# Cache-key loads tied to the products, a new panel order for the last head of group one, and output product 3 computed for each token group by itself

## The chip, the cores and the metric

The kernel runs on one core of a Trainium2 chip. Five engines work side by side, each with its own in-order instruction queue: TensorE (matrix products into the PSUM banks), VectorE, ScalarE, GpSimd and SyncE. SyncE only issues DMA transfers; ScalarE and GpSimd issue some as well. The metric is the device time of one execution in microseconds (us), as the median of several runs. Before the change it is 2291.69 us (three runs, 2291.46 to 2292.38).

## The reference

One inference step of a one-layer encoder with two kinds of heads. There are 1024 prompt frames of one new stream, and 16 new frames of each of 8 running streams (128 sample rows), with a width of 2048.

1. h = RMSNorm(x), and then one input projection of 2048 to 8 x 1024 columns: query, key, value and gate of eight stick-breaking heads, and query, key, value and gate of eight retention heads, 128 wide each.
2. Stick-breaking attention: z = q.k / sqrt(128); the weight of an earlier key is sigmoid(z) times the product of sigmoid(-z) over all keys that lie between it and the query. The prompt rows attend to earlier prompt rows. Each running stream attends to 1024 cached keys and values and to its own new rows.
3. Retention: rotary query and key, a decay per head, chunks with a carried 128 x 128 state; each running stream reads and updates its own state.
4. Each head's output is normalised, scaled, multiplied by SiLU(gate). Both groups of heads together (2048 wide) go through the output projection w_out (2048 x 2048). Then x + RMSNorm(out).

Everything is in fp32. The new keys, values and states are outputs too.

## The kernel before

**Precision.** A large product is done as three: operands are split into a rounded high part and the rest (`split`, L164: ScalarE makes the high part, L166, VectorE the rest, L167), and high x high, high x low and low x high are added up in PSUM. So each weight block costs a DMA load, one ScalarE and one VectorE instruction, and three matmuls for each tile or piece of tokens.

**Two token groups.** Group one (`gi` 0) holds prompt tiles 0 to 3 and the sample tile, 640 tokens; group two (`gi` 1) holds prompt tiles 4 to 7, 512 tokens. For each group the eight heads are done one after the other. A head has five pieces of projection: `rows` (values and gates of both branches, tokens on the partitions, L443), and four column panels of `project` (L386), each in four chunks of weights: 0 and 1 are query and key of stick-breaking, 4 and 5 those of retention. The list `order` at the end of the head loop says in which order they come: in group one `rows`, `ret_keys` (5), `ret_queries` (4), `attention` (0, then 1). The last head of group one is special: there `attention` calls `project_pair`, which does two panels chunk by chunk, and between the chunks `load_moving` brings in the inputs of group two, because the tiles of group one's inputs come free chunk by chunk when nothing after the pair reads them.

**Jobs and ticks.** Everything that is not a large product is a generator, a `Job`. After each product matmul step the code calls `tick`, which goes on with at most one job that is due; a job's `yield n` asks to be called again n ticks later. The constants `D_...` are such distances, for group one and group two. `drain(job)` runs ticks without products until the job is done. Three jobs go along with the heads: `ret_job` (retention), `sb_job` (stick-breaking of the prompt rows) and `sub` (`decode`, the running streams, only in group one). Each is drained at the place where its successor is made: `ret_job` in `ret_keys`, `sb_job` and `sub` in `attention` once the query panel is there.

**What orders the queues.** The instructions of each engine are ordered at compile time by a planner that takes the earliest instruction of the program whose inputs it reckons ready, so an instruction that depends on nothing can be placed far ahead of where it was written. `pin` and `tied` hold an instruction behind the last product written (`anchor[0]`) in this plan, without any wait on the chip.

**decode (L782).** The running streams' queries meet the cached keys in two sets of four key tiles (`kcT`, 512 KB each, loaded through GpSimd's queue, L794) and, once `rest` has the new key panel, the new keys. After sigmoid, masks, scan and turning the weights, eight tiles of cached values (`vc`, 512 KB each, on SyncE's queue, L834) follow, in two sets (L868). Keys and values share six buffers (`V_BUFS`). `KC_AHEAD` key tiles are loaded ahead, and the loop goes one tile further every `D_ZC` = 23 ticks. The loads of the keys hang on a free buffer only.

**Between the groups.** In the `attention` of group two's first head, `sub` is drained and the pool that holds these buffers is closed; a new pool takes its place for the attention keys of group two.

**retention (L885).** `ret_branch` turns the retention key around and then waits until `rows_in` holds the rotated query. The sample rows' part waits until a set of the decode's scores gives it a place (`with_scores`), at most `N_READ` x 2 ticks.

**Output products.** The output projection is done by a scheme with seven products of half the size (Strassen's): `LEFT[n]` and `RIGHT[n]` name the operands of product n, quarters of the mixed heads (`s_y`), of w_out, or sums of quarters that were made earlier (`s_s`, `s_b`). `left` loads and splits the left operand of a group in eight pieces; `kept(i)` puts the pieces of group one into the first or second quarter of the input tiles that are no longer read. `product(n, nh, groups, sample, ticks)` computes one half of the columns of product n: eight weight blocks, each used for two token tiles of every group named and, with `sample`, for the sample tile (L1182, L1185, L1186). `load_split` is called two blocks ahead in the order that `order_of` lists, and this list has to agree with the order of the calls. `bank` takes a PSUM bank from the rings acc0 and acc1 in turn; the projections use the same two. `collect` then adds the result to output areas. In the first scope, product 5 and one half of product 1 are computed for group one, while the last heads' jobs of group two go on; then the jobs are drained and the pools of the attention are closed. In the second scope come the rest of product 1 for group one, product 1 of group two, 2 for both, 5 for group two, and 3, 6, 7 and 4 for both. Group two's left operand of product 1 hangs on all eight stick-breaking heads, the last of which ends just before. The dictionary `then` says at which product the left operands of a later one begin to load.

Of the kernel before, what the change touches and what calls it, by code (L numbers as in the profile page):

```python
# [21 lines left out]
H = 8  # L22
# [26 lines left out]
D_OUT = 3  # L49
# [8 lines left out]
D_OP = 2  # L58
D_SUM2 = (4, 6, 26)
D_SUM3 = (3, 3, 6)  # L60
MR = 3
AHEAD = 2
HT = KT // 2
# [24 lines left out]
def tile_hybrid_step(  # L88
# [28 lines left out]
    nc = tc.nc  # L117
# [85 lines left out]
    anchor = [None]  # L203

    def tied(ins):

        if phase[0] == 0 and anchor[0] is not None:
            tc.add_manual_dep(
                ins.ins,
                anchor[0].ins.name,  # L210
                mybir.DependencyInfo(mybir.DependencyClass.NoSync, mybir.DependencyReason.SCHED_ONLY),
                reason="tied to the products",
            )

# [242 lines left out]
    with ExitStack() as s1:  # L457
# [324 lines left out]
        def decode(h, qs, rest):  # L782
# [9 lines left out]
            def load_k(m):  # L792
                kc = ip.tile([P, 2, 512], F32, name="kcT", tag="kv", bufs=V_BUFS)
                ready.append((kc, nc.gpsimd.dma_start(kc, cache_k[h, m // 4, m % 4])))  # L794
# [266 lines left out]
        for gi, g in enumerate(GROUPS):  # L1061
# [6 lines left out]
            for h in range(H):  # L1068
# [32 lines left out]
                def attention():  # L1101
                    nonlocal sb_job, sub, ip, loads
                    held = None
                    if (gi, h) == (0, 0):
                        acc = first[2]
                    elif (gi, h) == (0, H - 1):
                        loads = load_moving(after, 0, NB_TOK, from_h)
                        next(loads)
                        acc, held = project_pair(g, mov, (col(0, h), col(1, h)), loads)
                    else:  # L1110
                        acc = project(g, mov, col(0, h))
# [30 lines left out]
                    if gi == 1:  # L1142
                        kp = wp.tile([P, NB_TOK], F32, name="kpast", tag="mr", bufs=MR)
                        nc.sync.dma_start(kp, s_k[h])
                    acc = held or project(g, mov, col(1, h))
# [16 lines left out]
                if (gi, h) == (0, 0):  # L1162
                    order = ret_start, attention
                elif gi == 0 or h < H - 2:
# [25 lines left out]
        ring = [0]  # L1190
# [15 lines left out]
        order_of = iter([(n, nh, k) for n in (5, 1, 1, 2, 5, 3, 6, 7) for nh in range(2) for k in range(HT)] + [(4, 0, k) for k in range(HT)])  # L1206
# [48 lines left out]
        drain(nxt)  # L1255
        Job(collect(1, 0, product(1, 0, (0,), True, D_OUT)), 1)
        drain(ret_job)
# [4 lines left out]
    with ExitStack() as s3:  # L1262
# [78 lines left out]
        def all_of(made):  # L1341
# [5 lines left out]
            (1, 1): ((2, BOTH),), (2, 1): ((5, G1), (3, G0)), (5, 0): ((3, G1),), (3, 0): ((6, BOTH),),  # L1347
# [33 lines left out]
        for n, groups in ((1, G1), (2, BOTH), (5, G1), (3, BOTH), (6, BOTH), (7, BOTH)):  # L1381
# [168 lines left out]
```

## Time and profile before

| | |
|---|---|
| median of 3 runs | 2291.69 us |
| profiled execution | 2289.71 us |
| its span, from the first instruction to the last | 2288.0 us |
| mean granted TensorE clock | 0.991 |
| busy: TensorE, VectorE, ScalarE, GpSimd | 97%, 55%, 40%, 15% |
| DMA, mean over the span | 204 GB/s |

In the profile, PE is TensorE, PEld its weight loads, DVE VectorE, ACT ScalarE, POOL GpSimd, SP SyncE; a q behind a name (SPq) means the queue that issues, not the engine. A row of the order of time reads: start, length, engine, line, operation, out<-in, count, and in brackets the idle time before it with what ended it. A row of waits reads: who waited for whom, us in total, times, longest. Rows of one view that are not neighbours, and rows of different views in one fence, have a line of "..." between them.

### The profile page before, as it was taken

What the parts mean: (1) busy time and instruction counts of PE and PEld (TensorE: products, weight loads), DVE (VectorE), ACT (ScalarE), POOL (GpSimd) and SP (SyncE); (2) the same over time, 40 slices, a digit from 0 to 9 for tenths busy, and PEclk for the clock granted to TensorE, in tenths of its full rate; (3) what the DMA queues carried; (4) which work ended last, traced back from release to release, by engine and by line L of the source; (5) the groups of instructions that cost most, each with busy time, mean ns of one, the idle gap of its engine ahead of it and who ended that gap; (6) DMA issues with size and microseconds to landing.
All of it is one profiled execution on the core that took longest, in us unless ns stands there. A gap on an engine that the chain in (4) does not pass through costs nothing. (4 is left out here: it accounts for less than half of the span.)

```text
span 2288.0 us, 34700 instructions
## 1 busy us (share of the span) xinstructions
PE 2228.4 (97%) x12002; PEld 1889.0 (83%) x12002; DVE 1261.5 (55%) x2708; ACT 920.6 (40%) x1981; POOL 344.2 (15%) x577
## 2 busy tenths in 40 slices
PE   8999899999999999999989999999999999899998
PEld 7888779798888979888768888888888887678886
DVE  5335445354444545356546665756666666546567
ACT  6433233333333333334434343443334445445363
POOL 0021030111202021120202111120302212000020
PEclk9999999999999999999999999999999999999999
DMA  8566557585666658577668778878888767655586
GB/s 283 177 206 178 171 177 210 159 228 169 182 197 175 201 154 236 158 222 221 195 201 228 236 224 244 236 235 227 239 239 238 213 202 203 207 170 183 149 220 174
DMA packets 440048, 467.04 MB, mean 204 GB/s; under 512 B 182592, under 2 KB 298304, under 8 KB 439360
## 3 DMA queue, kind: packets, MB, share of 16 engines
q1 hardware_dynamic: 317632, 304.35, 45.7%
q0 software_dynamic: 28720, 78.41, 12.3%
q10 hardware_dynamic: 93520, 82.07, 11.6%
q8 instruction: 94, 1.54, 0.3%
q14 instruction: 82, 0.67, 0.1%
HBM read 363.77 MB, written 110.36 MB: 207 GB/s over the span
## 5 line engine op out<-in xcount | busy, mean ns | idle before, releaser
L386 PE MATMUL acc<-mh,wh 128*128 128x256 f32 (+2 forms) x1536 | 444.4, 340 | 19.9 <-ACT wh L166 19.8
L443 PE MATMUL accm<-whn,mh 128*128 128x512 f32 x1152 | 452.3, 393 | 0.1
L443 PE MATMUL accm<-wln,mh 128*128 128x512 f32 x1152 | 451.1, 392 | 0.9 <-DVE wln L167 0.9
L443 PE MATMUL accm<-whn,ml 128*128 128x512 f32 x1152 | 451.9, 392 | 0.0
L386 PE MATMUL acc<-ml,wh 128*128 128x256 f32 (+2 forms) x1536 | 447.3, 342 | 0.0
L386 PE MATMUL acc<-mh,wl 128*128 128x256 f32 (+2 forms) x1536 | 446.7, 341 | 0.3 <-DVE wl L167 0.3
L166 ACT ACTIVATE wh<-wr 128x512 fp32r<-128x512 f32 x392 | 246.8, 631 | 494.1 <-PE acc L386 159.0
L167 DVE TENSOR_TENSOR wl<-wr,wh 128x512 fp32r<-128x512 f32 x392 | 268.0, 687 | 307.1 <-ACT wh L166 289.6
L167 DVE TENSOR_TENSOR wln<-wrn,whn 128x512 fp32r<-128x512 f32 x256 | 175.6, 688 | 296.0 <-ACT whn L166 291.7
L166 ACT ACTIVATE whn<-wrn 128x512 fp32r<-128x512 f32 x256 | 160.8, 632 | 410.6 <-PE accm L443 268.9
L386 PEld LDWEIGHTS acc<-mh,wh 128*128 128x128 f32 x1536 | 285.1, 189 | 40.3 <-ACT wh L166 20.8
L386 PEld LDWEIGHTS acc<-mh,wl 128*128 128x128 f32 x1536 | 283.0, 189 | 25.2 <-issue 5.8
L386 PEld LDWEIGHTS acc<-ml,wh 128*128 128x128 f32 x1536 | 281.9, 190 | 19.0 <-DVE ml L172 0.4
L443 PEld LDWEIGHTS accm<-whn,mh 128*128 128x128 f32 x1152 | 216.4, 188 | 45.1 <-DVE kT L462 0.5
L443 PEld LDWEIGHTS accm<-wln,mh 128*128 128x128 f32 x1152 | 216.4, 188 | 44.6 <-DVE wln L167 1.7
L443 PEld LDWEIGHTS accm<-whn,ml 128*128 128x128 f32 x1152 | 216.5, 188 | 43.9 <-issue 0.8
L636 POOL DMA_DIRECT2D be<-s_be x128 | 94.2, 742 | 151.1 <-DMA s_be<-be 128.1
L672 DVE TENSOR_TENSOR_SCAN kp<-kp 128x1152 f32<-128x1152 f32 (+4 forms) x40 | 82.5, 2062 | 48.2 <-POOL kp L667 26.5
L1182 PE MATMUL a<-wh,mh 128*128 128x512 f32 x240 | 95.1, 397 | 6.4 <-ACT wh L166 3.4
L661 POOL TENSOR_SCALAR_AFFINE_SELECT kb<-kb 128x128 f32<-128x128 f32 x64 | 31.0, 498 | 437.4 <-ACT kb L655 436.6
L1186 PE MATMUL a<-wh,ml 128*128 128x512 f32 x240 | 94.9, 395 | 0.0
L1185 PE MATMUL a<-wl,mh 128*128 128x512 f32 x240 | 94.5, 394 | 0.0
(265 smaller groups left out, 2909.0 us busy)
## 6 DMA issues: line engine op xcount, KB each, us to landing
wr<-w_cols SPq DMA_DIRECT2D x256, 256.0 KB, 4.2
wrn<-w_rows SPq DMA_DIRECT2D x256, 256.0 KB, 3.5
kcT<-cache_k POOLq DMA_DIRECT2D x64, 512.0 KB, 7.6
vc<-cache_v SPq DMA_DIRECT2D x64, 512.0 KB, 5.3
wr<-s_b SPq DMA_DIRECT2D x80, 256.0 KB, 3.8
br<-w_out SPq DMA_DIRECT2D x64, 256.0 KB, 4.5
s_b<-br ACTq DMA_DIRECT2D x32, 512.0 KB, 4.7
wr<-w_out SPq DMA_DIRECT2D x64, 256.0 KB, 3.3
```

The source lines that it names most:

```text
L166: nc.scalar.activation(hi, src, AF.Copy),
L167: nc.vector.tensor_tensor(lo, src, hi.bitcast(F32), ALU.subtract),
L386: last = nc.tensor.matmul(a[:, :m], lhs[:, j, :], rhs[w][:, j, o : o + m], start=(w == 0 and j == 0 and n == 0), stop=(w == KT // WQ - 1 a ...
L443: anchor[0] = nc.tensor.matmul(banks[t], lhs[q][:, j, ts], rhs, start=(k == 0 and n == 0), stop=(k == KT - 1 and n == 2),)
L636: q.dma_start(raw[32 * i : 32 * i + 32, :].rearrange("p (k a) -> p k a", a=32), s[:, :, 32 * i : 32 * i + 32].rearrange("k (j b) a -> b (k ...
L661: nc.gpsimd.affine_select(blk, blk, pattern=[[-1, P]], base=0, channel_multiplier=1, compare_op=ALU.is_gt, fill=fill,)
L672: nc.vector.tensor_tensor_scan(rev, rev, rev, 1.0, ALU.mult, ALU.bypass)
L1182: ins = nc.tensor.matmul(a, hi[k][:, ts], wh, start=first, stop=False)
L1185: nc.tensor.matmul(a, hi[k][:, ts], wl, start=False, stop=False)
L1186: anchor[0] = nc.tensor.matmul(a, lo[k][:, ts], wh, start=False, stop=last)
```

## The change

Three parts, and what goes with them:

1. In `decode`, each load of a key tile is made to wait, on the chip, for the product matmul that was the last one written before it (`behind_products`).
2. In the last head of group one, the order is `rows`, `ret_keys`, `attention`. The query panel of stick-breaking is now computed by itself; then `project_pair` does the query of retention (4) together with the key of stick-breaking (1), with group two's inputs loaded meanwhile, and `ret_queries` rotates the former. So `decode` of this head is started ahead of the pair, `sb_job` and `sub` of the head before are drained there, and the rotated query comes after the pair.
3. Output product 3 is computed for group one (without the sample tile) in the first scope, between the first half of product 1 and the second, with its left operand in `kept(0)` in place of the second quarter; group two and the sample tile follow at its old place. Its weight blocks are loaded and split twice, 16 blocks more. The list of weight blocks follows. The ring of PSUM banks starts at 1 instead of 0.

```diff
+    def behind_products(ins):
+        tc.add_manual_dep(
+            ins.ins,
+            anchor[0].ins.name,
+            mybir.DependencyInfo(mybir.DependencyClass.Sync, mybir.DependencyReason.DATA),
+            reason="no sooner than its turn",
+        )
...
-                ready.append((kc, nc.gpsimd.dma_start(kc, cache_k[h, m // 4, m % 4])))
+                ld = nc.gpsimd.dma_start(kc, cache_k[h, m // 4, m % 4])
+                behind_products(ld)
+                ready.append((kc, ld))
...
-                    elif (gi, h) == (0, H - 1):
-                        loads = load_moving(after, 0, NB_TOK, from_h)
-                        next(loads)
-                        acc, held = project_pair(g, mov, (col(0, h), col(1, h)), loads)
...
+                    if (gi, h) == (0, H - 1):
+                        loads = load_moving(after, 0, NB_TOK, from_h)
+                        next(loads)
+                        queries, held = project_pair(g, mov, (col(4, h), col(1, h)), loads)
+                        ret_queries(queries)
                     acc = held or project(g, mov, col(1, h))
...
+                elif (gi, h) == (0, H - 1):
+                    order = rows, ret_keys, attention
...
-        ring = [0]
+        ring = [1]
...
-        order_of = iter([(n, nh, k) for n in (5, 1, 1, 2, 5, 3, 6, 7) for nh in range(2) for k in range(HT)] + [(4, 0, k) for k in range(HT)])
+        FIRST = ((5, 0), (5, 1), (1, 0), (3, 0), (3, 1), (1, 1))
+        LATER = (1, 2, 5, 3, 6, 7)
+        turns = [*FIRST, *((n, nh) for n in LATER for nh in range(2)), (4, 0)]
+        order_of = iter([(n, nh, k) for n, nh in turns for k in range(HT)])
...
+        mine[0, 3] = kept(0)
+        nxt = Job(left(0, 3, *mine[0, 3], wp, "mr", MR), D_OP)
         Job(collect(1, 0, product(1, 0, (0,), True, D_OUT)), 1)
+        drain(nxt)
+        for nh in range(2):
+            Job(collect(3, nh, product(3, nh, (0,), False, D_OUT)), 1)
         drain(ret_job)
...
-            (1, 1): ((2, BOTH),), (2, 1): ((5, G1), (3, G0)), (5, 0): ((3, G1),), (3, 0): ((6, BOTH),),
+            (1, 1): ((2, BOTH),), (2, 1): ((5, G1),), (5, 0): ((3, G1),), (3, 0): ((6, BOTH),),
...
-        for n, groups in ((1, G1), (2, BOTH), (5, G1), (3, BOTH), (6, BOTH), (7, BOTH)):
+        for n, groups in ((1, G1), (2, BOTH), (5, G1), (3, G1), (6, BOTH), (7, BOTH)):
```

## The prediction

> **What bounds the kernel now.** I read the front page first (busy shares, slices, clock), then the table of busy time by stretch at every place where TensorE pauses, then the waits and the order of time around each pause.
>
> ```profile
> span 2288.0 us, 34700 instructions
> PE 2228.4 (97%) x12002; PEld 1889.0 (83%) x12002; DVE 1261.5 (55%) x2708; ACT 920.6 (40%) x1981; POOL 344.2 (15%) x577
> ```
>
> TensorE is busy for 97% of the span. No matmul is added or taken away by the change, so all it can move is idle time and slow clock: 2288.0 - 2228.4 = 59.6 us idle, of which the start and the end are not touched. The stretches (columns: length; busy time and count of each engine; granted clock; DMA share; GB/s):
>
> ```profile
> core 0: us, PE busy (x) PEld busy (x) DVE busy (x) ACT busy (x) POOL busy (x), PEclk, DMA share, GB/s
> 235.00:245.00 10.00, 0.67 (x2) 0.67 (x3) 1.52 (x6) 1.23 (x3) 0.00 (x0) 0.61 0.97 271
> 245.00:255.00 10.00, 10.00 (x62) 10.00 (x62) 5.99 (x13) 2.78 (x7) 0.00 (x0) 0.88 0.46 142
> 1157.80:1170.70 12.90, 5.74 (x70) 2.80 (x69) 4.02 (x16) 4.07 (x9) 0.00 (x0) 0.80 0.77 229
> 1170.70:1178.70 8.00, 8.00 (x25) 6.35 (x26) 4.16 (x7) 2.16 (x5) 0.00 (x0) 0.68 0.71 230
> 1896.90:1900.00 3.10, 0.82 (x3) 0.43 (x3) 1.53 (x3) 2.01 (x5) 2.18 (x4) 0.90 1.10 201
> 1900.00:1903.00 3.00, 3.00 (x11) 2.42 (x10) 1.10 (x3) 0.56 (x2) 0.59 (x2) 0.53 1.05 302
> 1977.80:1984.60 6.80, 0.37 (x3) 0.04 (x1) 3.46 (x10) 2.87 (x8) 0.86 (x2) 0.76 0.94 281
> 1984.60:1988.20 3.60, 3.60 (x9) 2.86 (x10) 2.59 (x8) 1.80 (x6) 0.00 (x0) 0.51 0.66 251
> 2011.40:2015.20 3.80, 0.40 (x3) 0.05 (x1) 1.89 (x6) 3.11 (x7) 0.00 (x0) 1.00 0.86 247
> 2072.00:2092.00 20.00, 20.00 (x90) 16.57 (x89) 15.74 (x29) 16.10 (x38) 0.00 (x0) 1.00 0.71 225
> ```
>
> Five pauses, and behind four of them a stretch at a lower granted clock, which costs (1 - clock) x length. Each part of the change lies next to one or two of them, so I cost it pause by pause.
>
> **Pause one, 235 us: the keys' burst.** Head 0's decode frees the shared cache buffers at its two value products, and the loads of the next head's keys, bound to nothing, go out at once:
>
> ```profile
> 223.72 1.12 POOL L794 DMA_DIRECT2D kcT<-cache_k  x2 [23.58 <-PE pd L868]
> 228.50 2.20 POOL L794 DMA_DIRECT2D kcT<-cache_k  x4 [3.65 <-PE pd L868]
> ...
> 223.49 5.13 SPq L636 DMA_DIRECT2D ro<-s_rk  x4
> 228.72 7.91 SPq L636 DMA_DIRECT2D so<-s_o  x4
> 236.74 0.58 SPq L375 DMA_DIRECT2D wr<-w_cols  x1
> ...
> 1136.09 2.12 SPq L636 DMA_DIRECT2D ro<-s_rk  x4
> 1148.85 1.92 SPq L636 DMA_DIRECT2D so<-s_o  x4
> ```
>
> Six loads of 512 KB in 7 us; in the same time SyncE's queue spends 5.13 + 7.91 = 13.0 us on eight turn-in transfers that take it 2.12 + 1.92 = 4.0 us where no keys are loaded, and the weight block behind them is issued 9.0 us late.
>
> ```profile
> PE acc L386 <- ACT wh L166: 9.4, 1, 9.4
> ACT wh L166 <- DMA wr<-w_cols: 10.4, 1, 10.4
> ...
> wr<-w_cols SPq DMA_DIRECT2D x256, 256.0 KB, 4.2
> ...
> L166 ACT ACTIVATE wh<-wr 128x512 fp32r<-128x512 f32 x392 | 246.8, 631 | 494.1 <-PE acc L386 159.0
> L167 DVE TENSOR_TENSOR wl<-wr,wh 128x512 fp32r<-128x512 f32 x392 | 268.0, 687 | 307.1 <-ACT wh L166 289.6
> ```
>
> With each key load tied to the product that stands ahead of it, the next head's keys cannot start before that head's decode, a whole head later. Then the weights go out at 236.74 - 9.0 = 227.7, land 4.2 later (231.9), are split by 233.2 (0.63 + 0.69), and TensorE, which ran dry just before 235, need not wait. Worth 10.00 - 0.67 = 9.3 idle and 0.12 x 10 = 1.2 of clock, 10.5; at worst nothing, if the order of SyncE's queue alone does it. I take 9.5, near the upper end because the same instructions are priced with and without the burst.
>
> What the tie costs in each head: the load waits in GpSimd's in-order queue, and behind it stand the masks (affine_select) and the turn-outs of the attention rows, for whose result VectorE and then TensorE wait.
>
> ```profile
> DMA to landing us min/median/max: 4.1/7.6/11.1
> ...
> 989.05 0.45 PE L386 MATMUL acc<-mh,wh 128*128 128x256 f32 x2
> 1057.12 0.40 PE L443 MATMUL accm<-whn,mh 128*128 128x512 f32 x1
> ...
> POOL s_be L629 <- DVE be L673: 18.0, 2, 16.1
> ```
>
> Four column panels of 48 ticks last from 989.05 to 1057.12, 17.0 us each, 0.35 us a tick. The last key tile of a set is issued three steps of 23 ticks ahead of its product, 24 us; it lands in 7.6, at most 11.1 (first row). So 13 us of room cover it; cost 0 to 1, counted below.
>
> **Pause two, 1158 us: the last head's decode.** It starts only when the pair of its query and key panels is done, so its end falls into group two, where the pool with its buffers has to be closed.
>
> ```profile
> 1158.16 2.80 PE L868 MATMUL pd<-vc,kp 128*32 128x256 f32 x48
> 1162.62 0.64 PE L868 MATMUL pd<-vc,kp 128*32 128x256 f32 x8 [1.66 <-DMA vc<-cache_v]
> 1166.64 0.66 PE L742 MATMUL z<-kh,qh 128*128 128x384 f32 x1 [1.78 <-issue]
> 1170.70 0.79 PE L386 MATMUL acc<-mh,wh 128*128 128x512 f32 x1 [2.76 <-ACT wh L166]
> ...
> ACT kh L166 <- PE pd L868: 9.9, 1, 9.9
> ...
> 1027.00:1057.00 30.00, 28.53 (x200) 28.16 (x200) 21.47 (x50) 14.38 (x31) 0.00 (x0) 1.00 0.84 259
> ```
>
> TensorE waits for the values themselves, ScalarE stands 9.9 us on the next pool's first tile until the value products are done, and the weight block behind it is late. The new panel order (key of retention, query of attention, then the pair) starts this decode two panels earlier, 2 x 17.0 = 34 us; its value products then come near 1158 - 34 = 1124, in the midst of products, as in all other heads. Worth 12.9 - 5.74 = 7.2 idle and 0.32 x 8 = 2.6 of clock, 9.7 (the 5.74 us of matmul stay). Against it: up to six of its key loads, 3.1 MB, now run under the pair, where 30 us at 259 GB/s already move 7.8 MB at a share of 0.84. In proportion 0.84 x 10.9 / 7.8 = 1.17, 5.2 us too much if nothing gives; but the group's inputs for later are among the 7.8, so most of it can wait. I take 8.5; ends 4.5 and 9.7. The retention query comes last now, so this head's retention starts about 68 ticks later; it still ends about when the next head's retention key panel asks for it. The attention before it must be finished one panel earlier; its remaining steps are transfers and VectorE work, no products.
>
> **Pauses three to five: the tail.** Three edits meet here: the bank ring starts at 1, product 3 of group one runs ahead of the last piece of product 1, and its weights are loaded twice.
>
> ```profile
> 1899.61 0.77 PE L1182 MATMUL a<-wh,mh 128*128 128x512 f32 x1 [2.28 <-DVE rq L490]
> 1937.08 1.16 PE L769 MATMUL pa<-vo,kp 128*128 128x128 f32 x8 [1.15 <-DVE kp L732]
> 1984.59 0.77 PE L1182 MATMUL a<-wh,ah 128*128 128x512 f32 x1 [6.43 <-issue]
> ...
> 1975.91 0.33 ACTq L709 DMA_DIRECT2D s_y<-so  x1
> ...
> PE a L1182 <- ACT wh L166: 4.6, 3, 3.4
> ```
>
> Ring: the first output product takes acc0, acc1, acc0; its third bank is the one from which VectorE still rotates the last retention query (first row). Starting at 1 it takes acc1, acc0, acc1, and waits for nothing. Worth 3.10 - 0.82 = 2.3 and 0.47 x 3 = 1.4 of clock, 3.7; at worst 0, if TensorE arrives earlier only to wait longer for the attention rows (1.15 at 1937). I take 2.7. [...]
>
> Product 3: two halves of 8 blocks x 2 tiles x 3 matmuls, 96 at 20.00 / 90 = 0.22 us, 21.3 us. They are put ahead of the point (1977.8) where TensorE waits for group two's left operand, which hangs on the last attention head: stored at 1975.91, its reload and split let TensorE go at 1984.6. Now TensorE gets there near 1977.8 + 21.3 - 2.7 = 1996.4, 11.8 us after. The whole pause goes: 6.80 - 0.37 = 6.4 and 0.49 x 3.6 = 1.8, 8.2. Next late is what comes behind it: the operands of product 2, at 2011 (3.8 - 0.4 = 3.4; three waits for split weights, 4.6 in all). They shared the DMA queues with the catching up; that goes, but 16 operand pieces still have to land during two short products. I take 2.0 of 4.6; ends 0 and 4.6.
>
> Cost of the split: 16 more weight blocks, each 0.63 us of ScalarE, 0.69 of VectorE and 256 KB, against 2 x 3 x 0.22 = 1.33 us of matmul. Group two's product 5 has the same two tiles per block and runs without a pause (2072 to 2092, 0.71 share). So 0; bare, without matmul over it, 16 x 1.32 = 21.1. The left operand of product 3 moves from product 2's time into product 1's, eight 128-KB loads on SyncE's queue. For this, the tie and an order of the queues drawn anew I put 2.5 us of new small waits (0 to 6).
>
> **Sum.** 9.5 + 8.5 + 2.7 + 8.2 + 2.0 - 2.5 = 28.4 us. 2288.0 - 28.4 = 2259.6 us of span. The profiled execution took 2289.71, the median of the runs is 2291.69, 3.7 above the span: 2263.3.
>
> **Rivals.** (1) The queue's order, not the burst, makes pause one: SyncE stands still on value loads before it anyway. The 13.0 against 4.0 us speaks against it. 9.5 comes back: 2272.8. (2) Under the pair the key loads take the engines from the weights: 5.2 us paid, so the boundary gives 4.5 instead of 8.5: 2267.3. [...] The stretched turn-ins agree; 3.1 MB spread over 30 us is far from such a burst. (3) The tail's loads stay late: only half of 8.2 and nothing of 2.0: 2269.4. For it: DMA shares of 0.86 to 0.94 there. (4) Slower: the tied key load stands in GpSimd's queue behind a turn-out that waits for VectorE, up to 16.1 us (the row above). 24 - 16.1 - 11.1 = -3.2: TensorE waits 3.2 us at each of 16 key sets, 51 us: 2314. It decides from 28.4 / 16 = 1.8 us a set. Against it: turn-outs and key loads lie in one order of ticks, and a hold-up of 16 together with a landing of 11.1 would have to meet every time.
>
> **How the numbers follow.** The forecast has 0.58 (own range 2256 to 2268), rival 1 0.14, 2 0.09, 3 0.11, two of these together 0.03 (about 2280), 4 0.05. All gains in full and no new waits, 10.5 + 9.7 + 3.7 + 8.2 + 4.6 = 36.7, give 2255; the upper end takes in rivals 1 to 3 and two together: 2254 to 2280. 0.2%, 4.6 us, is about what a measurement of this kernel tells from no change. Faster by more 0.90, within it 0.05 (several of the rivals in part), slower 0.05.
>
> **What would show it.** In the changed profile: no six key loads in a row near 224 to 230 but single ones through the head, eight turn-ins there in about 4 us, and no wait of 9.4 for a split weight block; the last value products of group one before 1140, and no pause of ScalarE on the next pool; no wait on the rotated query at the start of the output products; group two's first block of product 1 without a pause; clock rows at 1.00. The forecast is wrong if new waits of TensorE for key tiles or attention rows appear in every head, if weights are late under the pair, or if a pause of several us stands between the two-tile blocks of product 3.

## The result, and the profile after

The changed kernel takes **2274.32 us** (median of four executions, 2272.97 to 2282.22) against 2292.03 for the kernel before in the same comparison: a ratio of 0.9926, 95% interval 0.9912 to 0.994. So it is faster by 17.7 us. The forecast was 2263.3 with a range of 2254 to 2280: right in sign and range, with 28.4 us promised where 17.7 came. Measured again in a later comparison, the same kernel gave 0.9943 (0.9931 to 0.9955).

The profiled execution is the slowest of the four: its span is 2280.5 us at a mean granted clock of 0.992, while the other three have 2271.2 to 2273.9 us at 0.994 to 0.995. What follows about places is read from that one execution; why executions of one kernel differ so much is told in the last section.

The front page after, first the span, then the busy row:

```profile
span 2280.5 us, 34787 instructions
...
PE 2229.1 (98%) x12002; PEld 1891.4 (83%) x12002; DVE 1272.2 (56%) x2724; ACT 926.8 (41%) x1995; POOL 343.7 (15%) x577
```

Idle time of TensorE went from 59.6 to 2280.5 - 2229.1 = 51.4 us. The stretches after, at the five places that the prediction costed (columns as in its table; the added lines shift the line numbers, so L386, L490 and L868 of before are L394, L498 and L878 after):

```profile
236.40:239.00 2.60, 0.47 (x3) 0.28 (x3) 1.42 (x8) 0.74 (x2) 0.00 (x0) 1.00 0.64 213
239.00:245.00 6.00, 6.00 (x40) 5.86 (x41) 3.79 (x6) 2.08 (x4) 0.00 (x0) 1.00 0.61 195
1045.00:1050.10 5.10, 2.56 (x15) 1.07 (x7) 3.86 (x7) 3.38 (x7) 0.53 (x1) 1.00 0.88 297
1050.10:1056.90 6.80, 5.40 (x14) 4.36 (x15) 3.93 (x8) 4.42 (x7) 0.00 (x0) 0.50 0.87 277
1117.00:1121.80 4.80, 2.33 (x21) 1.24 (x20) 1.63 (x4) 1.98 (x4) 0.00 (x0) 1.00 0.77 149
1121.80:1128.60 6.80, 6.63 (x30) 5.38 (x34) 4.68 (x14) 2.18 (x6) 0.00 (x0) 0.50 0.24 80
1141.00:1145.70 4.70, 2.19 (x10) 1.50 (x8) 3.29 (x7) 0.63 (x1) 0.00 (x0) 1.00 0.53 115
1145.70:1152.50 6.80, 5.92 (x14) 4.70 (x15) 3.86 (x9) 1.81 (x3) 0.00 (x0) 0.50 0.68 160
...
1975.00:1995.00 20.00, 20.00 (x90) 16.57 (x89) 11.72 (x20) 8.98 (x17) 1.62 (x4) 1.00 0.86 267
...
2020.00:2026.30 6.30, 3.88 (x15) 2.30 (x13) 4.74 (x13) 4.12 (x12) 0.00 (x0) 1.00 0.74 226
2026.30:2033.10 6.80, 4.76 (x11) 3.79 (x12) 3.91 (x7) 4.08 (x8) 0.00 (x0) 0.50 0.76 254
...
1158.00:1172.00 14.00, 14.00 (x76) 11.94 (x75) 8.62 (x27) 5.66 (x18) 0.00 (x0) 1.00 0.38 115
```

The pauses at 1158 and at 1978 are gone: 1158 to 1172 and 1975 to 1995 are now full at a clock of 1.00. The one at 235 is shorter, the one in front of product 2 is still there, and between the groups three new pauses have come, each with half clock behind it.

To compare kernels by place I use one measure for all: for each pair of neighbouring matmuls, the distance of their starts less the usual back-to-back distance of the first one's shape in the trace at full clock (0.2265 us for 512 columns, 0.175 for 384, 0.117 for 256), summed by stretch. It holds idle time and slow clock together. Its sums, 109.1 us before and 101.6 after, differ by 7.5, as the spans do (2288.0 and 2280.5).

| lost time, us, by stretch | before | after | again | promised | came (after, again) |
|---|---|---|---|---|---|
| 200 to 300 (pause one) | 14.7 | 6.2 | 8.9 | 9.5 | 8.5, 5.8 |
| 990 to 1200 (between the groups) | 21.9 | 26.0 | 24.5 | 8.5 | -4.1, -2.6 |
| 1880 to 2060 (pauses three to five) | 25.4 | 19.0 | 16.7 | 12.9 | 6.4, 8.7 |
| everything else | 47.2 | 50.4 | 52.0 | -2.5 | -3.2, -4.8 |

The profiled pair differs by 7.5, the medians by 17.7. The profiled execution before (2289.71) lay a little below its median, the one after far above it. Places are compared within this table, totals by the medians.

**Pause one.** The order of time around 235 after, and the row of the key loads' landing:

```profile
224.52 0.82 SPq L844 DMA_DIRECT2D vc<-cache_v  x2
225.44 4.37 SPq L644 DMA_DIRECT2D ro<-s_rk  x4
229.91 3.11 SPq L644 DMA_DIRECT2D so<-s_o  x4
233.12 7.08 SPq L383 DMA_DIRECT2D wr<-w_cols  x5
...
251.04 1.78 POOL L802 DMA_DIRECT2D kcT<-cache_k  x3 [49.39 <-PE acc L394]
...
kcT<-cache_k POOLq DMA_DIRECT2D x64, 512.0 KB, 4.9
...
SPq L844 <- PE pd L878: 6.9, 1, 6.9
...
PE acc L394 <- ACT wh L166: 2.1, 1, 2.1
```

The burst is gone: the next head's first three key loads leave together at 251.04, the other five singly, and the median of all heads lands in 4.9 us instead of 7.6. The eight turn-ins (loads that bring a tile back from memory in turned order) take 4.37 + 3.11 = 7.5 us, not 13.0 and not the 4.0 of the forecast, and the weight block leaves at 233.12, not 227.7. The wait row for SyncE shows what the sum had passed over: the queue stands 6.9 us at two value loads whose buffers the decode still holds, and all the rest stands behind them. The kernel before has the same wait in its waits of SyncE's queue, as rival (1) said:

```profile
SPq L834 <- PE pd L868: 6.5, 1, 6.5
```

**Between the groups.** Waits, and rows in order of time, after:

```profile
PE accm L451 <- DVE rq L498: 3.9, 2, 2.1
...
DVE kb L740 <- DMA kb<-s_be: 5.5, 2, 5.1
...
PE pSs L996 <- DVE st L1000: 2.6, 1, 2.6
...
PE acc L394 <- DVE rk L498: 3.4, 1, 3.4
...
1048.41 0.48 PE L451 MATMUL accm<-whn,mh 128*128 128x512 f32 x1 [1.80 <-DVE rq L498]
...
1122.42 0.68 DVE L497 TENSOR_TENSOR sw<-sw,sinT 128x512 f32<-128x512 f32 x1
...
1128.00 3.06 PE L878 MATMUL pd<-vc,kp 128*32 128x256 f32 x48
...
1144.28 0.84 DVE L715 STREAM_TRANSPOSE rk<-ro 128x640 f32<-128x640 f32 x1
...
1145.74 0.69 DVE L498 TENSOR_TENSOR rk<-acc,cosT 128x512 f32<-128x512 f32 x1
```

The transposition (L715 in the rows above) in the kernel before, in order of time:

```profile
1120.52 0.84 DVE L707 STREAM_TRANSPOSE rk<-ro 128x640 f32<-128x640 f32 x1
```

The decode's value products do come early (1128, forecast 1124). The closeness is in part luck: TensorE reaches the first product of group two's rows at 1048.41 instead of 1057.12, 8.7 us that come from earlier pauses and that the forecast left out. Counted from there, the value products moved from 101.0 us to 79.6, by 21 us and not by 34. But: (i) the next head's rows wait twice for PSUM banks that hold the pair's retention query, which VectorE is still rotating; (ii) near 1119 VectorE stands 5.1 us at the turn-in of the previous attention's weights, and the state products of retention wait for the instruction behind it; (iii) head 7's retention, which uses the rotated key's buffer for its last transposition, reaches that transposition at 1144.28 instead of 1120.52, and the next head's rotated key, into the same buffer, goes on only behind it at 1145.74, though its first step (L497) is there from 1122.42 on, while TensorE needs its banks.

**The tail.** Rows after, in order of time, and waits:

```profile
1999.56 12.59 SPq L1212 DMA_DIRECT2D wr<-w_out  x11
2012.20 1.10 SPq L325 DMA_DIRECT2D mr<-s_y  x2
...
PE rs L899 <- DVE rq L499: 1.7, 1, 1.7
...
PE a L1195 <- ACT ml L1255: 2.5, 1, 2.5
...
PE a L1195 <- ACT wh L166: 5.5, 3, 3.7
```

The first output product no longer waits for a bank; in the same place the retention scores now wait 1.7 us for the same rotated query. A bank wait of 2.5 us near 1940 is new in size (the pause there was 0.93 us before), and product 2's pause stays: its first operand loads stand behind eleven weight loads that take 12.59 us of SyncE's queue.

### The profile page after: what moved, and what is told of

It is laid out like the page before. It is cut to its first block, busy times and chain, and to the rows that moved or that the text cites. A ratio compares the mean times of both kernels' runs of the same rounds, so it can differ in the third digit from the quotient of the medians.

```text
span 2280.5 us, 34787 instructions
## 1 busy us (share of the span) xinstructions
PE 2229.1 (98%) x12002; PEld 1891.4 (83%) x12002; DVE 1272.2 (56%) x2724; ACT 926.8 (41%) x1995; POOL 343.7 (15%) x577
## 3 DMA queue, kind: packets, MB, share of 16 engines
q0 software_dynamic: 28720, 78.41, 12.6%
## 4 chain that ended last, share of the span: by engine, by line
PE 83%; DMA 6%; issue 4%; DVE 4%; ACT 2%; SPq 1%; ACTq 0%; DVEq 0%; POOL 0%; POOLq 0%
PE accm L451 34%; PE acc L394 27%; PE a L1195 4%; PE a L1199 4%; PE a L1198 4%; PE pa L777 2%; PE z L750 2%; PE zc L817 1%; PE pd L878 1%; DMA wr<-w_out 1%; DMA ro<-s_rk 1%; DMA mr<-s_s 1%; PE pa L917 1%; PE rs L899 1%; ACT wh L166 1%
## 5 line engine op out<-in xcount | busy, mean ns | idle before, releaser
L394 PE MATMUL acc<-mh,wh 128*128 128x256 f32 (+2 forms) x1536 | 445.0, 340 | 12.6 <-ACT wh L166 9.3
L394 PE MATMUL acc<-mh,wl 128*128 128x256 f32 (+2 forms) x1536 | 447.3, 342 | 0.3 <-DVE wl L167 0.3
L394 PE MATMUL acc<-ml,wh 128*128 128x256 f32 (+2 forms) x1536 | 446.4, 341 | 0.0
L166 ACT ACTIVATE wh<-wr 128x512 fp32r<-128x512 f32 x408 | 256.2, 631 | 466.3 <-PE acc L394 168.2
L167 DVE TENSOR_TENSOR wl<-wr,wh 128x512 fp32r<-128x512 f32 x408 | 278.8, 687 | 274.1 <-ACT wh L166 259.9
L394 PEld LDWEIGHTS acc<-mh,wh 128*128 128x128 f32 x1536 | 285.3, 190 | 31.9 <-ACT wh L166 9.5
L394 PEld LDWEIGHTS acc<-mh,wl 128*128 128x128 f32 x1536 | 283.2, 189 | 26.5 <-issue 6.8
L394 PEld LDWEIGHTS acc<-ml,wh 128*128 128x128 f32 x1536 | 282.7, 190 | 20.3 <-issue 1.2
L802 POOL DMA_DIRECT2D kcT<-cache_k x64 | 34.8, 546 | 588.3 <-PE acc L394 404.9
```

The lines of the kernel that those rows point to most:

```text
L166: nc.scalar.activation(hi, src, AF.Copy),
L167: nc.vector.tensor_tensor(lo, src, hi.bitcast(F32), ALU.subtract),
L394: last = nc.tensor.matmul(a[:, :m], lhs[:, j, :], rhs[w][:, j, o : o + m], start=(w == 0 and j == 0 and n == 0), stop=(w == KT // WQ - 1 a ...
L802: ld = nc.gpsimd.dma_start(kc, cache_k[h, m // 4, m % 4])
```

## The experiments

**The same kernel again**, as the yardstick of the next three runs.

> The changed kernel once more, unchanged, for a second profiled execution: its four times so far run from 2272.97 to 2282.22 us and the profiled one was the longest. Theory (places): at the boundary of the groups stand three new pauses (banks held by the rotated query near 1046, a sample state near 1119, the rotated key near 1143 us), 8 us of idle and as much slow clock; in an execution of 2273 at least one of them is missing, and the pause near 235 us and the one near 1978 us are gone in both. Rival (spread): the 9 us between executions lie over the whole span, in transfers of every head, and no single pause differs by more than 1 us.

Measured: 2281.16 us, ratio 0.9943 (0.9931 to 0.9955). The three pauses between the groups are there again (lost time 24.5 us), with a fourth of 2.15 us for a value tile at 1137, and so is the one near 235; they belong to the kernel and not to one execution. But the profiled execution was a long one again (2282.84 us), so which pauses a short one lacks stays open. Between these two executions of one kernel the lost time differs by 2.7, 1.5 and 2.3 us at the three places of the table. In what follows a difference of under 3 us between two single executions therefore tells nothing by itself.

**Each part alone on the kernel before.** First the tie:

```diff
-                ready.append((kc, nc.gpsimd.dma_start(kc, cache_k[h, m // 4, m % 4])))
+                ld = nc.gpsimd.dma_start(kc, cache_k[h, m // 4, m % 4])
+                behind_products(ld)
+                ready.append((kc, ld))
```

> Only the tie of the key loads (part 1), all else as before. Theory (places): acts at 235 us alone, where 10.5 us were lost and 2.3 are left in the changed kernel: 2292 - 8 = 2284, and the stretches of the other heads, the boundary and the tail stay as before. Rival (queue order): the pause at 235 is made by the order of SyncE's queue and is merely another order in the changed kernel: 2292, with the pause still there. Rival (queue held): the tie slows each head: above 2292.

Measured: 2288.34 us, ratio 0.9983 (0.9972 to 0.9994). Lost time at 200 to 300 falls from 14.7 to 7.7, at 990 to 1200 it rises from 21.9 to 26.7: there the key loads run in step with group two's inputs, and TensorE waits 3.7 us at 1059 for a weight split that stands behind such an input on ScalarE. Of the 7.0 us that the tie gains at head 0 it gives back 4.8 between the groups.

Then the panel order:

```diff
-                        acc, held = project_pair(g, mov, (col(0, h), col(1, h)), loads)
+                        queries, held = project_pair(g, mov, (col(4, h), col(1, h)), loads)
+                        ret_queries(queries)
...
+                    order = rows, ret_keys, attention
```

> Only the new panel order of the last head of group one (part 2). Theory (places): the pause of 9.8 us at 1158 goes, the three new pauses of the boundary come, 10 to 20 us with the slow clock: 2292 to 2302, so nothing gained or a loss. Rival (tie at fault): the new pauses come from key loads that run tied under the pair; without the tie they are absent and the time is 2292 - 9 = 2283.

Measured: 2294.2 us, ratio 1.0005 (0.9994 to 1.0016): nothing. The stretch 990 to 1200 rises from 21.9 to 25.3. All three new pauses are there without the tie, so they come from the order. The value products of group one's last head start at 1134.71, 23 us ahead of the 1158.16 before, and not 34.

Then product 3's split with the ring's start:

```diff
-        ring = [0]
+        ring = [1]
...
+        for nh in range(2):
+            Job(collect(3, nh, product(3, nh, (0,), False, D_OUT)), 1)
```

> Only the split of output product 3 with the bank ring started at 1 (part 3). Theory (places): the pause of 8.2 us near 1978 goes, 2 to 4 us come back as waits for collected banks and for operands of product 2: 2292 - 5 = 2287, at best 2283. Rival (interaction): the tail's gain needs nothing of the other parts but loses the boundary's: 2279.

Measured: 2285.65 us, ratio 0.9968 (0.9957 to 0.9978); lost time in the tail from 25.4 to 20.3. It is the largest single gain. The three parts alone sum to -0.44% (0.9983, 1.0005 and 0.9968 give 0.9956 multiplied); the whole gave 0.9943 in the same comparison. The intervals of the sum and of the whole overlap; the parts add up nearly, and none undoes another.

**Tie and split without the order:**

> Parts one and three (with the ring), the panel order of before. The panel order alone measured 1.0005, so if its three new pauses are worth as much as the old one it took away, this kernel stands where the whole change stands, about 2281 (ratio 0.994). If the order loses once the key loads are tied (in the tie alone the stretch 990 to 1200 lost 26.7 us against 21.9, in the whole change 24.5 to 26.0), the two parts do not add up and this kernel comes out between 2277 and 2280. By the prediction's sum, where the order is worth 8.5, it would be 8.5 slower than the whole change, near 2290.

Measured: 2283.32 us, ratio 0.9957 (0.9945 to 0.9969). Between the groups it loses 25.4 us, no less than the whole change with 26.0 and 24.5. The wait that the order was to take away is its largest there (row of the waits of this kernel):

```profile
ACT kh L166 <- PE pd L878: 10.4, 1, 10.4
```

So with the tie the order is neither gain nor loss at its own place: it pays for one large pause with three small ones. The whole kernel stands a little better than this one (0.9926 and 0.9943), but the lost time differs in stretches that the order doesn't touch (21.0 against 19.0 and 16.7 in the tail), so what the order is worth in the whole stays open, between nothing and some 0.3%.

**Is it the rotated key's buffer at 1143?** The first head of group two computes its retention query before its retention key:

```diff
+                elif (gi, h) == (1, 0):
+                    order = rows, ret_queries, ret_keys, attention
```

> The whole change, and in the first head of group two the retention query panel ahead of the retention key panel. Theory: the 3.4-us pause near 1143 comes from head 7's retention, which now ends late and still holds the buffer of the rotated key that the next head's key panel needs; 17 us more of room take the pause and the slow clock behind it away: 3.5 + 0.5 x 3.4 to 6.8, so 5 to 7 us less than the whole change, near 2275, and no wait of a projection on the rotated key there. Rival: it is the buffer of the rotated query or the row of vector work that is late, and the pause only moves to the next panel: within 1.5 us of the whole change.

Measured: 2279.41 us, ratio 0.9941 (0.9929 to 0.9953); lost time between the groups 19.6 us. The wait of 3.4 has shrunk to 0.7:

```profile
PE acc L394 <- DVE rk L498: 0.7, 1, 0.7
...
1151.14 0.84 DVE L715 STREAM_TRANSPOSE rk<-ro 128x640 f32<-128x640 f32 x1
```

The transposition comes even later (1151.14), and the rotated key still goes on only behind it, at 1152.61; but TensorE needs its banks later now, and waits 0.7 instead of 3.4. The theory holds at the place, with 5 to 6 us less of lost time. The total doesn't show it: 0.9941 lies within the intervals of the whole change (0.9926 and 0.9943).

**Is it the rotation that holds the banks at 1046?** The key first in the pair, its scaling ahead of the rotation:

```diff
-                        queries, held = project_pair(g, mov, (col(4, h), col(1, h)), loads)
-                        ret_queries(queries)
+                        held, queries = project_pair(g, mov, (col(1, h), col(4, h)), loads)
...
+                    if (gi, h) == (0, H - 1):
+                        ret_queries(queries)
```

> The whole change, with the key of stick-breaking as the first and the query of retention as the second panel of the pair, the key's scaling ahead of the rotation. Theory: the two pauses near 1046 and 1049 (1.9 and 2.3 us, and 3.4 to 6.8 us of half clock behind them) come from the rotation, which holds the first two banks longer (two copies on ScalarE and three instructions on VectorE a piece, one scratch buffer for both pieces) than a scaling would; with the key first the next head's rows get their first two banks after one instruction each: 3 to 6 us less than the whole change. Rival: the rows' third and fourth bank wait as long instead: within 1.5 us of the whole change.

Measured: 2276.59 us, ratio 0.9923 (0.991 to 0.9936); lost time between the groups 20.0 us. Of the two pauses the first is gone, as the theory said, and the second is left, so what remains is the third and fourth bank, as the rival said:

```profile
PE accm L451 <- DVE rq L498: 2.8, 1, 2.8
...
1044.00:1050.00 6.00, 6.00 (x37) 3.85 (x37) 3.84 (x6) 3.88 (x6) 0.53 (x1) 1.00 0.89 281
```

Most of the 4.5 to 6.0 us of lost time less is clock: between the groups this execution has 6.8 us of half clock, the two of the whole change 20.5 and 13.7. By the last section that depends on the execution, so the edit's own worth isn't shown beyond the first pause, and the total (0.9923) is that of the whole change.

**Is product 2's pause only late loads?** Its operands start one half product earlier:

```diff
-            (1, 1): ((2, BOTH),), (2, 1): ((5, G1),), (5, 0): ((3, G1),), (3, 0): ((6, BOTH),),
+            (1, 0): ((2, BOTH),), (2, 1): ((5, G1),), (5, 0): ((3, G1),), (3, 0): ((6, BOTH),),
```

> The whole change, and the sixteen left-operand pieces of output product 2 start to load one half product earlier (with the first half of group two's product 1 in place of the second). Theory: the pause at the start of product 2 (1.4 + 0.7 + 3.8 and up to 3.4 of slow clock in the changed kernel, which the prediction put at 2.0 gained) is plain lateness of these loads behind eleven weight blocks on SyncE's queue: 5 to 8 us less than the whole change. Rival: the queues are full there and the loads only push the weight blocks of product 1 back: the pause moves to product 1, within 1.5 us of the whole change.

Measured: 2285.39 us, ratio 0.9954 (0.9939 to 0.9969). No gain, as the rival said: the loads leave earlier, and now weight blocks stand behind operand pieces. Pauses of 1.1, 2.6, 1.1 and 2.7 us between 2006 and 2020 take the place of the ones at 2004 and 2024.

**Both edits between the groups.**

> The whole change with both edits at the boundary: the key of stick-breaking first in the pair, and head (1,0)'s retention query panel ahead of its retention key panel. Theory: the pauses near 1046 and 1143 have separate causes (banks held by a rotation; a buffer held by head 7's retention), so what each edit gave in its own run (the stretch 990 to 1200 at 20.0 and 19.6 us instead of 24.5 to 26.0) adds up: 14 to 16 us in that stretch, ratio 0.990 to 0.991, a median near 2272. Rival: both edits only give the same vector work more room and share one gain: the stretch stays at 19 to 20, ratio near 0.992.

Measured: 2272.84 us, ratio 0.9913 (0.9894 to 0.9932); lost time there 21.1 us, and 17.8, 20.9 and 17.2 in the three kernels below that keep both edits. The rival was nearer: each edit alone gave 19.6 and 20.0, and together they lose 19.3 in the mean of the four, no real addition. What is left is a pause of 2.65 us at 1052, where ScalarE is late with an input of group two, and pause (ii), which neither edit touches and which has the longest half clock behind it (10.2 us in this execution):

```profile
DVE kb L740 <- DMA kb<-s_be: 5.5, 1, 5.5
...
PE pd L870 <- DVE kp L867: 2.9, 1, 2.9
```

The waiting instruction on VectorE is the same as in the whole change; this time the decode's turned weights stand behind it.

**Product 2's operands on GpSimd's queue**, on top of both:

```diff
-                pin(nc.sync.dma_start(r, s_y[gi][src[1] * H + h][:, src[2] * 256 : src[2] * 256 + 256]))
+                pin((nc.gpsimd if n == 2 else nc.sync).dma_start(r, s_y[gi][src[1] * H + h][:, src[2] * 256 : src[2] * 256 + 256]))
```

> The kernel with both boundary edits, and the sixteen left-operand loads of output product 2 issued by GpSimd's queue instead of SyncE's. Theory: the pause at the start of product 2 comes from the order of SyncE's queue: eleven weight loads stand there waiting for their buffers (13.3 us in one row) and the operand loads stand behind them. On GpSimd's queue, which does nothing then, they start some 8 us earlier: the pauses near 2000 and 2018 (2.0 + 4.1 us and 5 us of half clock's cost) go, 4 to 8 us less than the kernel with both boundary edits. Rival: the DMA engines are what is short there (share 0.80 to 0.87); the weight blocks come later instead and TensorE waits as long: within 1.5 us.

Measured: 2269.51 us, ratio 0.9898 (0.988 to 0.9915). The pause in front of product 2 is gone, which says that the queue's order made it. But one at the start of group two's product 1 has grown:

```profile
1998.86 0.80 PE L1198 MATMUL a<-wh,ah 128*128 128x512 f32 x1 [2.86 <-ACT wh L166]
...
2000.00:2020.00 20.00, 20.00 (x85) 16.37 (x85) 14.21 (x30) 13.42 (x29) 4.81 (x9) 0.94 0.85 278
```

In the tail as a whole 13.2 us are lost against 13.5, so theory and rival each have a half, and the 3.3 us between the medians are within both intervals.

**The retention scores 16 ticks later**, on top of both boundary edits:

```diff
+            if (gi, h) == (1, H - 1):
+                yield 16
```

> The kernel with both boundary edits, and the last head's retention scores asked for 16 ticks later, some 3.5 us. Theory: the ring's new start only passed on the wait for the last rotated query: the instruction that frees the bank stands in VectorE's queue behind an operand piece whose load is late, and the retention scores, issued next, need the same result. Asked for later, they find it done: the pause of 1.9 to 2.7 us near 1890 goes, 2 to 4 us less than the kernel with both boundary edits. Rival: the fourth bank of the output products, which is the one that the rotation still reads, takes the wait over: within 1 us.

Measured: 2275.58 us, ratio 0.9916 (0.9896 to 0.9935), no gain. A pause stays at 1895, on the same rotated query. But the edit did less than the 3.5 us expected of it: the scores stand behind 18 matmuls of the output products where they stood behind 14, some 0.9 us, and TensorE's wait went from 1.82 to 1.11 us. Why 16 ticks came to so little isn't known, and a request that is late enough was not tried. What makes the query late is in VectorE's rows of this run:

```profile
1894.90 0.43 DVE L167 TENSOR_TENSOR ml<-mr,mh 128x256 fp32r<-128x256 f32 x1 [1.85 <-ACT mh L166]
1895.24 0.68 DVE L498 TENSOR_TENSOR rq<-acc,cosT 128x512 f32<-128x512 f32 x1
```

The step of the rotation that frees the bank (L498) stands behind an operand piece for which VectorE waits 1.85 us.

**The last two value loads on GpSimd's queue**, on top of both boundary edits and the operands' queue:

```diff
-                ld = nc.sync.dma_start(vc, cache_v[h, k])
+                ld = (nc.gpsimd if k >= V_BUFS else nc.sync).dma_start(vc, cache_v[h, k])
```

> The kernel with both boundary edits and product 2's operand loads on GpSimd's queue, and each decode's last two value loads issued by GpSimd's queue too. Theory: what is left of the pause at 235 us (2.2 us in every kernel with the tied key loads, with 0 to 6.8 us of half clock behind it) comes from the order of SyncE's queue: it stands 6.9 us at a value load whose buffer is not free yet, with the eight turn-ins and the weight block behind it. With the value loads elsewhere these go out some 5 us sooner, the pause goes, and the stretch 200 to 300 falls from 7.7 to 4 to 5: 2 to 4 us less. Rival: the turn-ins wait for their own inputs at that time and the weight block is as late as before: within 1 us; or the value loads, now behind the next head's key loads or turn-outs in GpSimd's queue, come late to their products: a wait for a value tile in the stretch 300 to 990, some us slower.

Measured: **2264.94 us**, ratio 0.9866 (0.9846 to 0.9886), the best of all. Lost time at 200 to 300 falls from 7.7 to 4.9:

```profile
214.27 6.69 SPq L383 DMA_DIRECT2D wr<-w_cols  x4
221.05 3.91 SPq L644 DMA_DIRECT2D ro<-s_rk  x4
225.06 5.21 SPq L644 DMA_DIRECT2D so<-s_o  x4
...
222.88 1.14 POOL L844 DMA_DIRECT2D vc<-cache_v  x2 [22.83 <-PE pd L878]
...
229.15 0.64 PE L878 MATMUL pd<-vc,kp 128*32 128x256 f32 x8 [0.71 <-DMA vc<-cache_v]
230.75 0.64 PE L878 MATMUL pd<-vc,kp 128*32 128x256 f32 x8 [0.97 <-DMA vc<-cache_v]
...
200.00:240.00 40.00, 38.32 (x300) 35.54 (x299) 19.69 (x51) 10.56 (x24) 1.19 (x3) 1.00 0.77 186
```

The turn-ins take no less time (9.1 us), yet TensorE waits for no weight block: four blocks now go out ahead of the turn-ins, from 214.27 on, since no value load stands in the queue before them. The value tiles themselves are 0.7 and 1.0 us late. So the rest of pause one was the standing queue, not the length of the turn-ins. In the total this edit's own 0.3% is within the intervals (0.9898 before it); the two moves to GpSimd's queue together, from 0.9913 to 0.9866, are clear of them.

## Why the prediction was right, and where it was wrong

**Pause one (9.5 promised, 5.8 to 8.5 came).** The mechanism was right: the burst stretched the turn-ins, and the tie takes it away. Two terms were off. The turn-ins cost 7.5 us and not the 4.0 of the row that served as the price; that row came from another head. And rival 1, at 0.14, was half true: the queue's order alone kept a pause of 2.1 us, as the last experiment shows, and the 6.5 us for which SyncE stood at the value loads were in the profile before.

**Pause two (8.5 promised, a loss of 2.6 to 4.1 came).** This is the step that failed. The value products came near their place, though by 21 us of their own instead of 34, and no pause of TensorE hangs on the next pool any more (ScalarE still stands 3.2 us there, 9.9 before). What failed is the sentence that retention "still ends about when the next head's retention key panel asks for it". Counted from the first product of group two's rows, head 7's transposition came at 63.4 us before (1120.52 - 1057.12) and at 95.9 after (1144.28 - 1048.41), 32 us later where 68 ticks make 24. The panel's first rotation step had not moved with it: 72.7 before (L489 at 1129.82) and 74.0 after (1122.42). So TensorE lost 3.4 us and half clock. The sentence on the previous attention, "its remaining steps are transfers and VectorE work, no products", was true and hid the fault: VectorE stood 5.1 us at such a transfer, everything behind it in its queue waited as long, and TensorE's products hung on that. And the forecast did not ask which banks the pair leaves occupied: a rotation frees them later than a scaling (two waits of the next rows, 3.9 us; one of 2.8 in the run that scales first). The new pauses leave TensorE idle for 4.0 (1.80 and 2.15), 2.6 and 3.4 us, 10.0 together, against 7.2 in the old ones (1.66, 0.96, 1.78 and 2.76), with three spells of half clock of 6.8 us against one of 10.2. The table's 4.1 is less than that makes, because small waits of the old order went too (1.35 us at 1036.77, for one).

**The ring (2.7 promised, at most the clock came: 1.00 from 1895 to 1903, 0.53 behind the pause before).** The forecast named the case itself: "at worst 0, if TensorE arrives earlier only to wait longer" — only the successor was another one, the retention scores, which need the same rotated query: 2.28 us of waiting became 1.7. The run with the scores put off shows what makes the query late: the rotation stands behind an operand piece in VectorE's queue.

**Product 3 (8.2 promised).** Right: the stretch from 1975 to 1995 is full at a clock of 1.00, and group two's first block finds its operand. That the 16 extra blocks cost nothing was right as well. The split paid elsewhere: the pause at 1940 grew from 0.93 to 2.6 us (1.7 in the kernel run again), and the kernel with part three alone has it too (a wait of 2.5). ScalarE, which has to empty the banks there, first stands 1.61 us at a piece of product 1's left operand (`mr<-s_y`, 1940.60). The pieces that the split added (`mr<-s_s`) are issued only from 1939.15 on and aren't what it stands at; why the piece of product 1 comes later than before isn't shown. The promised 2.5 of small waits contain that.

**Product 2's operands (2.0 promised, about 0 came).** The pause was put down to shared DMA queues that would be relieved. It is the order in SyncE's queue: operand loads behind eleven weight loads that wait for their buffers. That order the change did not touch. (Of the 4.6 us named as the upper end, 0.94 lay at 1991, in group two's product 1.) Rival 3, "nothing of 2.0", had this half.

**New small waits (-2.5).** -3.2 and -4.8 in the stretches that the change should not touch: about right, at the lower end, but in part chance: a pause near 113 us that all three executions have (1.84 us before, 2.59 after) was followed by 3.4 us of half clock in both after and by none in the one before. **Rival 4**, the tied load held up in GpSimd's queue, did not come at all: 24.1 us lost from 300 to 990 against 24.8 before.

By the table the profiled pair falls 28.4 - 7.5 = 20.9 us short: 12.6 at pause two, which cost instead of giving, 6.5 in the tail, 1.0 at pause one and 0.7 elsewhere. The medians fall only 10.7 short, because the profiled execution after lay 7.9 us above its median and the one before 2.3 below. Of the 7.9, some 5.7 are half clock (0.992 against 0.994 to 0.995; 0.0025 x 2275 = 5.7 us).

## What to carry to other kernels

A panel moved within a head moves every buffer and bank that its result sits in: ask for each moved result which buffer it shares, who needs that next, and what stands behind its producer on an in-order engine. A queue that stands at a load for a busy buffer delayed everything behind it here (SyncE's, 6.9 us): moving two groups of loads to another queue took the ratio from 0.9913 to 0.9866 here, more than any one part of the change gave alone. When a wait is taken away by renaming the resource, look at whether the late producer has a second reader just behind.

## What the runs showed of the hardware that was not expected

**Equal pauses cost unequal clock.** In every kernel with the tie and SyncE's old order, ten profiled executions, the pause near 235 is the same 2.12 or 2.13 us. Behind it the clock stayed full in the profiled execution after (1.00 in the mean from 200 to 300), was half for 3.4 us in six (0.98) and for 6.8 us in three (0.97), `again` among them. Two rows of the profiled execution after, then two of `again`:

```profile
234.30:237.71 3.41, 1.88 (x13) 1.50 (x11) 2.62 (x11) 0.85 (x3) 0.00 (x0) 1.00 0.89 267
237.71:241.13 3.42, 2.19 (x14) 2.06 (x15) 2.34 (x5) 2.19 (x4) 0.00 (x0) 1.00 0.24 73
...
234.87:238.28 3.41, 1.27 (x9) 0.89 (x7) 2.76 (x11) 0.30 (x3) 0.00 (x0) 1.00 0.81 257
238.30:245.10 6.80, 6.20 (x23) 6.20 (x24) 2.50 (x4) 2.11 (x4) 0.00 (x0) 0.50 0.60 186
```

A pause of 1.98 us near 1890 was followed by nothing in the kernel with both boundary edits (clock 1.00 from 1880 to 2060) and by 3.4 us of half clock in the last one (0.99). So a pause of about two us cost from 0 to 3.4 us more than its length here (half of up to 6.8). The changed kernel's four executions go from 2271.2 us at a clock of 0.994 to 2280.5 at 0.992; by the estimate above, half clock makes some 5.7 of the 7.9 us by which the longest lies above the median. The spells last 3.4, 6.8 or 10.2 us, whole multiples of 3.4 (10.24, 10.24, 3.41, 6.83 and 3.41 before, 3.41 and four times 6.83 after, apart from the one at the end of the span).

The clock records of the two profiled executions, before and after, show what this goes with. In each of them all eleven changes of the clock lie within 1 ns on one grid with steps of 3.413 us, and the step just ahead of each drop is one in which TensorE does little. Ahead of the five drops that come before the end of the span it is busy for 0.56, 1.28, 1.33, 0.24 and 0.31 us before (7 to 39% of the step) and for 1.20, 0.94, 0.97, 0.94 and 1.57 us after (28 to 46%). The least busy steps with a full clock behind them, the first 20 us left out, have 1.80 us before (53%) and 1.56, 1.59 and 1.80 us after (46, 47 and 53%). A drop and the step ahead of it in the kernel before, then the same after, then a step after that had no drop behind it:

```profile
233.70:237.12 3.42, 0.56 (x3) 0.30 (x2) 2.13 (x10) 0.00 (x0) 0.00 (x0) 1.00 1.05 369
237.12:247.36 10.24, 3.03 (x11) 3.03 (x12) 2.65 (x4) 2.44 (x4) 0.00 (x0) 0.50 0.84 223
...
2022.89:2026.30 3.41, 1.57 (x6) 0.86 (x5) 2.33 (x7) 2.45 (x7) 0.00 (x0) 1.00 0.78 235
2026.30:2033.13 6.83, 4.79 (x11) 3.80 (x12) 3.91 (x7) 4.08 (x8) 0.00 (x0) 0.50 0.76 254
...
1940.97:1944.38 3.41, 1.56 (x7) 1.30 (x8) 1.54 (x3) 2.95 (x7) 0.78 (x1) 1.00 1.03 197
1944.38:1947.79 3.41, 3.41 (x17) 2.83 (x16) 1.31 (x3) 0.96 (x3) 0.00 (x0) 1.00 1.08 260
```

The rows of the pause near 235 are such steps, but for the last: in the execution after, a border of the grid splits the pause (1.88 and 2.19 us busy, 55% and 64%), and in `again` nearly all of it lies in one step (1.27 us, 37%). So where a pause falls on the grid goes with what it costs in these executions: the ones of 2.59 us near 113 and 2.6 near 1119 in the changed kernel were followed by half clock, and one of 2.45 near 1940, which a border splits, was not, nor was one of 1.74 near 1896. Why 1.57 us at 2022.89 was followed by half clock and 1.56 at 1940.97 was not isn't shown.
